# Two plain feed-forward pairs per layer, a state reload tied behind the last weight load, and one attention output product for both kv pairs, in a two-layer decoder step

## The chip, the cores and the metric

The kernel runs on one core of a Trainium2 chip. The metric is the device time of one execution in microseconds (us); three runs of the kernel before took 3076.03, 3079.45 and 3083.96 us, so its median is 3079.45 us. TensorE (PE) multiplies, VectorE (DVE), ScalarE (ACT) and GpSimd (POOL) work on the results, and SyncE (SP) issues the transfers; "PEld" is the loading of weights into TensorE, and "SPq" the queue of transfers that SyncE fills. Each engine works through its own instructions strictly in the order in which they stand, so an instruction that waits holds up all those behind it on the same engine.

## What is computed

One step of a two-layer decoder on 1024 prompt rows, 8 x 8 sample rows and 16 meta rows, 1104 columns in the kernel's transposed layout. Layer 0 is a state-space mixer with a feed-forward part, layer 1 is windowed attention with a feed-forward part, on 1088 columns (the meta rows have dropped out).

```python
def sq_relu_mlp(h, norm_w, w_up, w_down):
    return h + jnp.square(jax.nn.relu(rmsnorm(h, norm_w) @ w_up)) @ w_down

# layer 0
ym, conv_m, ssm_m = mamba_mixer(hm, zero_conv, zero_ssm, *prm)
...
# layer 1: keys and values shared, then queries, attention, output product
hp = hp + swa_prompt(q_p, k_p, v_p, k_meta, v_meta, attn_sinks[j]) @ w_o[j]
hs = hs + swa_sample(q_s, k_s, v_s, cache_k_win, cache_v_win, k_meta, v_meta, attn_sinks[j]) @ w_o[j]
...
hp = sq_relu_mlp(hp, mlp_norm_w[layer], w_up[layer], w_down[layer])
```

The model width is 1024, the hidden width of the feed-forward part 4096; there are 16 query heads and 4 key/value heads.

## The kernel before

**Three products for one.** Every float32 operand is split into a high part and a rest (`wh`, `wl` for weights, `xh`, `xl` for data), and `mm3` (L177 to L179) issues three matmuls for each 128-row slice. A weight comes in by a transfer into a `raw` buffer (two of them), ScalarE casts it to the high part (L162, or L853 for half-size pieces), GpSimd subtracts to get the rest (L163, L854); in layer 1 GpSimd first multiplies the queries' weights and the plain pairs' weights with a norm's weights (L160). There are six weight tiles `w` of 4 KB for each partition: a 128 x 1024 weight takes two of them, one for each part.

**Columns.** Work on the 1104 (1088) columns goes by three chunks of 384, 384 and 336 (320) columns. `S` holds the high parts and the rests of the stream, `g` names the single PSUM banks of the usual products, taken in a ring.

**Up projection.** The 4096 hidden columns are made in 16 pairs `f` of 2 x 128. A plain pair (`plain_up`) multiplies 8 slices x 3 matmuls for two halves and three chunks, 144 matmuls, and each result `g` is read out (ScalarE L833 in layer 0, VectorE L835 with the norm's factor in layer 1), squared (L836) and stored to DRAM (`r_d`, in layer 1 `r_e`). A block pair (`up_pair`) uses seven block products in place of eight, as Strassen's scheme does, on quarters of the columns (276 or 272 wide): 7 x 2 x 4 x 3 = 168 matmuls into four two-bank PSUM tiles `ma`, `mb`, `mc`, `md`, which VectorE (L882) and ScalarE combine. The weights of a block pair are sums that VectorE forms in `s` (L863, L869). The data of a block pair are sums too, which `sides` makes once a layer: differences of four slices over a quarter of the columns on VectorE (L795), the high part by ScalarE (L817) and the rest by VectorE (L818), six of them into tiles `T` and the others over the normed data in `S`. Those over `S` can be written only when no plain product reads that part of `S` any more. Before, pair 0 is plain and pairs 1 to 15 are block pairs.

**Between mixer and up projection in layer 0.** The last mixer products add into `hh` (L724), the squares of `hh` are summed in `acc`, a small product over all partitions (`ms`, L223 and L226) gives the norm's factor `rs` (two ScalarE functions, L234 and L235), then VectorE scales `hh` (L786), ScalarE writes the high part to `S` (L787) and VectorE the rest (L788), chunk by chunk. The plain pair starts on chunk 0 while chunk 2 is still being normed.

**Attention and its output product.** `attention` goes through chunks 0, 2, 1; for each, through two kv pairs `pr` and four query groups `r`; a step makes the next step's queries, then scores, softmax and weighted values for every 128 columns, with results in `ah` and `al` (eight buffers each). When four groups are done, four `out_unit` calls are noted down in `outs` and run at a later step; each loads one output weight, multiplies four slices (12 matmuls) into each of two `g` banks, and reads each bank out: two VectorE additions of the old `S` (L1319, L1320), a ScalarE cast (L1321) and a GpSimd or VectorE subtraction (L1322) back into `S`. For the second kv pair the sum goes on through `stream` (store to `h_e`, sum of squares in `acc`, L116). So each of the 24 column pieces (8 slices x 3 chunks) is read out twice, once for each kv pair. The last chunk's sum is kept in `X`; the other two chunks of `X` are loaded back from `h_e` (L126) and scaled with their norm factors (L136).

**Down projection.** Eight blocks of four 128-row slices; a block's data are read from `r_d`/`r_e` into `S` (L939), split on the chip (L944 cast, L945 rest), and its results are added to `hh` (L724). `hh` is reloaded from DRAM for this (L1487 in layer 0, L1555 in layer 1, eight transfers).

**Order.** The program is written in the order of the functions, and a scheduler at build time then fixes for each engine in which order its instructions stand, by dependences, priorities and free buffers. SyncE's transfers are fixed in the same way.

## Time and profile before

| what | value |
|---|---|
| median of three runs | 3079.45 us |
| the profiled execution | 3083.63 us, its span 3081.9 us |
| TensorE, mean granted clock | 0.979 |
| VectorE busy | 1751.6 us (57%) |
| ScalarE busy | 1377.2 us (45%) |
| GpSimd busy | 1253.1 us (41%) |
| moved by transfers | 305.87 MB, mean 99 GB/s |

The table is read from the top: the span is the profiled execution without what lies around its first and last instruction (1.7 us here). No engine but TensorE is busy for more than 57% of the span, but the shares differ from stage to stage: the up and down projections run from about 1090 to 1800 us (layer 0) and from about 2290 us to the end (layer 1), attention from about 1890 to 2276 us. Busy shares of TensorE are those of overlapping matmuls; how many matmuls stand in a stretch tells more.

### The profile page before, as it was taken

Reading aid. Unit: us, or ns where it says so; the run is one execution under the profiler, and the core shown is the slowest. Engines: PE = TensorE matmul, PEld = TensorE weight load, DVE = VectorE, ACT = ScalarE, POOL = GpSimd, SP = SyncE. Lnnn points to the kernel's source line nnn. Section 1 sums busy time; section 2 is a strip of 40 time slices with the busy share of each in tenths; the row PEclk is TensorE's granted clock in tenths of the full one; section 3 lists DMA queues with packets and bytes.
Section 4 is the critical chain, followed back from the end, with each engine's and each line's share of the span. In section 5 each row is a group of like instructions: output and inputs, shape, how many; then the busy total and the mean of one; then the engine's idle time right before and its main releaser. Section 6 shows DMA issues by size and latency. Waiting matters only on the chain.

```text
span 3081.9 us, 49051 instructions
## 1 busy us (share of the span) xinstructions
PE 2929.1 (95%) x19222; PEld 2796.9 (91%) x19222; DVE 1751.6 (57%) x3008; ACT 1377.2 (45%) x2606; POOL 1253.1 (41%) x1079
## 2 busy tenths in 40 slices
PE   6999999989999989999999999999987999999998
PEld 4988888879999979999999998887876999999998
DVE  5777877775555584332433356877886433423335
ACT  5455555555445554444221136656644544402113
POOL 4466666653333234443112145574532444312122
PEclk8999999999999999999999999999998999999999
DMA  3244444443222224234422212123232323512221
GB/s 128 68 118 119 119 115 117 128 134 130 73 67 75 78 76 132 89 112 154 149 100 78 71 42 63 64 90 99 80 108 85 107 96 114 194 55 99 107 71 66
DMA packets 189761, 305.87 MB, mean 99 GB/s; under 512 B 27528, under 2 KB 137480, under 8 KB 187464
## 3 DMA queue, kind: packets, MB, share of 16 engines
q1 hardware_dynamic: 189528, 302.72, 31.1%
q8 instruction: 151, 2.47, 0.3%
q14 instruction: 82, 0.67, 0.1%
HBM read 232.72 MB, written 70.92 MB: 99 GB/s over the span
## 4 chain that ended last, share of the span: by engine, by line
PE 49%; DVE 8%; ACT 3%; issue 3%; POOL 1%; DMA 1%; SPq 0%; DVEq 0%; ACTq 0%; POOLq 0%
PE g L178 9%; PE g L177 9%; PE g L179 9%; PE md L179 2%; PE md L178 2%; PE md L177 2%; PE mc L179 2%; PE mc L178 2%; PE mc L177 2%; PE ma L177 2%; PE ma L179 2%; PE ma L178 2%; PE mb L179 1%; PE mb L178 1%; PE mb L177 1%
## 5 line engine op out<-in xcount | busy, mean ns | idle before, releaser
L178 PE MATMUL g<-S,w 128*128 128x384 f32 (+2 forms) x2808 | 940.3, 335 | 9.5 <-DVE S L1322 4.7
L177 PE MATMUL g<-S,w 128*128 128x384 f32 (+2 forms) x2808 | 937.2, 334 | 11.4 <-DVE hh L724 3.8
L179 PE MATMUL g<-S,w 128*128 128x384 f32 (+2 forms) x2808 | 935.7, 333 | 0.0
L163 POOL TENSOR_TENSOR w<-raw,w 128x1024 fp32r<-128x1024 f32 x184 | 445.9, 2424 | 933.1 <-ACT w L162 866.3
L177 PEld LDWEIGHTS g<-S,w 128*128 128x128 f32 x2808 | 529.3, 188 | 19.6 <-DVE hh L724 4.0
L178 PEld LDWEIGHTS g<-S,w 128*128 128x128 f32 x2808 | 530.1, 189 | 17.3 <-DVE S L1322 5.3
L724 DVE TENSOR_TENSOR hh<-hh,g 128x384 f32<-128x384 f32 (+2 forms) x552 | 287.5, 532 | 445.0 <-PE g L179 444.3
L179 PEld LDWEIGHTS g<-S,w 128*128 128x128 f32 x2808 | 530.5, 189 | 6.2 <-issue 3.5
L162 ACT CAST w<-raw 128x1024 fp32r<-128x1024 f32 x184 | 192.5, 1046 | 603.6 <-PE g L178 575.1
L854 POOL TENSOR_TENSOR w<-s,w 128x512 fp32r<-128x512 f32 x120 | 166.3, 1390 | 332.3 <-ACT w L853 332.3
L532 DVE SCALAR_TENSOR_TENSOR fm<-xp,cv,fm 128x1024 f32<-128x1024 f32 x96 | 165.4, 1724 | 31.7 <-ACT fm L513 31.2
L854 POOL TENSOR_TENSOR w<-raw,w 128x512 fp32r<-128x512 f32 x90 | 123.1, 1369 | 95.1 <-ACT w L853 64.5
L177 PE MATMUL ma<-S,w 128*128 128x276 f32 (+1 forms) x480 | 139.7, 291 | 15.1 <-DVE n L835 13.8
L179 PE MATMUL ma<-S,w 128*128 128x276 f32 (+1 forms) x480 | 139.4, 290 | 0.0
L178 PE MATMUL ma<-S,w 128*128 128x276 f32 (+1 forms) x480 | 139.1, 290 | 0.0
L177 PE MATMUL g<-gh,w 128*128 128x384 f32 (+1 forms) x384 | 126.9, 332 | 2.4 <-DVE gt L696 1.1
L178 PE MATMUL g<-gl,w 128*128 128x384 f32 (+1 forms) x384 | 126.6, 330 | 0.0
L179 PE MATMUL g<-gh,w 128*128 128x384 f32 (+1 forms) x384 | 126.2, 330 | 0.0
L585 ACT ACTIVATE dec<-ab,acs 128x128 f32<-128x128 f32 (+1 forms) x288 | 90.8, 387 | 67.8 <-PE y L594 64.3
L863 DVE TENSOR_TENSOR s<-raw 128x512 f32<-128x512 f32 x60 | 50.1, 854 | 118.8 <-DMA raw<-in_w_up_dram 90.0
L177 PEld LDWEIGHTS ma<-S,w 128*128 128x128 f32 x480 | 91.1, 190 | 15.7 <-DVE n L835 14.1
L630 POOL TENSOR_TENSOR yt<-yt,yo 128x256 f32<-128x256 f32 (+1 forms) x72 | 68.2, 948 | 88.6 <-DVE yt L627 82.2
(390 smaller groups left out, 6891.8 us busy)
## 6 DMA issues: line engine op xcount, KB each, us to landing
raw<-in_w_up_dram SPq DMA_DIRECT2D x64, 512.0 KB
raw<-in_w_down_dram SPq DMA_DIRECT2D x64, 512.0 KB
raw<-in_w_in_dram SPq DMA_DIRECT2D x48, 512.0 KB
ab<-acs_d SPq DMA_DIRECT2D x64, 256.0 KB
S<-r_e SPq DMA_DIRECT2D x28, 544.0 KB
S<-r_d SPq DMA_DIRECT2D x24, 552.0 KB
raw<-in_w_q_dram SPq DMA_DIRECT2D x24, 512.0 KB
raw<-in_w_o_dram SPq DMA_DIRECT2D x24, 512.0 KB
```

The source lines that it names most:

```text
L162: nc.scalar.copy(out=wh, in_=raw)
L163: nc.gpsimd.tensor_tensor(out=wl, in0=raw, in1=wh.bitcast(F32), op=ALU.subtract)
L177: mm(out=out, lhsT=wh, rhs=xh, start=(first and k == 0), stop=False)
L178: mm(out=out, lhsT=wh, rhs=xl, start=False, stop=False)
L179: mm(out=out, lhsT=wl, rhs=xh, start=False, stop=(k == n - 1))
L532: nc.vector.scalar_tensor_tensor(out=acc[:, :SEQ], in0=xp[:, k:k + SEQ], scalar=cv[:, j, k:k + 1], in1=acc[:, :SEQ], op0=ALU.mult, op1=ALU ...
L585: nc.scalar.activation(out=dec[:n, h, :n], in_=ab[:n, h, :n], func=AF.Relu, scale=-1.0, bias=self.acs[:n, t, 4 * g + h:4 * g + h + 1])
L630: nc.gpsimd.tensor_tensor(out=yt[:, :, :no], in0=yt[:, :, :no], in1=yo[:, :, :no], op=ALU.add)
L724: nc.vector.tensor_tensor(out=hv, in0=hv, in1=pt[:, :n], op=ALU.add)
L854: nc.gpsimd.tensor_tensor(out=t[:, 1], in0=src, in1=t[:, 0].bitcast(F32), op=ALU.subtract)
L863: add = lambda a, b, op: (lambda t: (nc.vector.tensor_tensor(out=t, in0=a, in1=b, op=op), t)[1])(self.wsum([P] + sh))
```

## The change

1. In each layer pairs 0 and 1 are plain, and `up` starts at pair 2. A plain pair now yields once a chunk instead of once a result.
2. In layer 1 the tiles `T` come from one pool of six (before, two pools of three on the two sides of the memory), and the steps of `sides` stand elsewhere in the program: those of the first half of the blocks after the first chunk of pair 0, the others behind pair 0 and ahead of pair 1.
3. `hh` is reloaded by `load_stream`, with an ordering edge behind the last `raw` weight load of the up projection.
4. For chunks 0 and 2 the output product is made once for both kv pairs: an `out_unit` loads two weights (four of the six weight tiles) and multiplies eight slices (24 matmuls) into each bank, and the bank is read out once. Chunk 1 stays as it was. The noted units now also run one at a time at the steps of the first kv pair. `ah` and `al` have twelve buffers.

```diff
-                yield
+            yield
...
-        self.nc.sync.dma_start(out=t, in_=view)
+        self.last_raw = self.nc.sync.dma_start(out=t, in_=view).ins
...
-            for f in range(1, 16):
+            for f in range(2, 16):
...
+    def load_stream(self, big, h_d):
+
+        with self.tc.issue_after(self.last_raw):
+            for u in range(KT):
+                self.nc.sync.dma_start(out=big[:, u], in_=h_d[:, u])
...
-            if r == 3:
-                while outs:
+            if r == 3 or pr == 0 and outs:
+                for _ in range(len(outs) if r == 3 else 1):
                     self.out_unit(*outs.pop(0))
...
-                oc, opr = (c, pr) if sp is None else (2, sp)
-                outs += [(oc, chs[oc][1], opr, v, [a[oc, 4 * opr + q] for q in range(4)], xs, stream)
-                         for v in range(4)]
+                oc, prs = (c, (pr,)) if sp is None else (2, (sp,))
+                if oc != 1:
+                    prs = prs[0] * (0, 1)
+                if prs:
+                    outs += [(oc, chs[oc][1], prs, v, [a[oc, 4 * e + q] for e in prs for q in range(4)], xs, stream)
+                             for v in range(4)]
...
-        wh, wl = self.wunit(self.i["w_o"][pr, v], 4, 256)
+        ws = [self.wunit(self.i["w_o"][pr, v], 4, 256) for pr in prs]
+        last = prs[-1] == 1
...
-            self.mm3(pt, [(wh[:, k, ms], wl[:, k, ms]) for k in range(4)], [tuple(e[:, :n] for e in x) for x in a])
+            self.mm3(pt, [(wh[:, k, ms], wl[:, k, ms]) for wh, wl in ws for k in range(4)],
+                     [tuple(e[:, :n] for e in x) for x in a])
...
+                    for _ in self.plain_up(0, 1, dict(enumerate(CH)), rd):
+                        pass
...
-            for u in range(KT):
-                nc.sync.dma_start(out=big[:, u], in_=h_d[:, u])
+            self.load_stream(big, h_d)
...
-                for i in (1, 2, 3):
-                    step(i, 0)
...
                 next(plain)
+                for i in (1, 2, 3):
+                    step(i, 0)
                 stream.norm(1)
+                for _ in plain:
+                    pass
                 for i in (1, 2, 3):
                     step(i, 1)
-                for _ in plain:
+                for _ in self.plain_up(1, 1, {c: chs[c] for c in (0, 2, 1)}, rd, stream.rs, pre):
                     pass
```

Three places show what the scheduler made of it.

TensorE in layer 0, where the plain products end; before, `g_11404` and `g_11433` are the last results of pair 0, with weights `w_11244` and `w_11250`, and the first block product `ma` follows:

```order
L178 MATMUL g_11404<-S_90,w_11244 128x336
L179 MATMUL g_11404<-S_90,w_11245 128x336
L178 MATMUL g_11433<-S_90,w_11250 128x336
L179 MATMUL g_11433<-S_90,w_11251 128x336
L177 MATMUL ma_11512<-S_90,w_11509 128x276
L178 MATMUL ma_11512<-S_90,w_11509 128x276
```

Now pair 1 follows, whose results are `g_11503` and `g_11532` (chunks 0 and 1), with its own weights `w_11470` and `w_11464`:

```order
L178 MATMUL g_11404<-S_90,w_11244 128x336
L179 MATMUL g_11404<-S_90,w_11245 128x336
L178 MATMUL g_11433<-S_90,w_11250 128x336
L179 MATMUL g_11433<-S_90,w_11251 128x336
L177 MATMUL g_11503<-S_90,w_11470 128x384
L178 MATMUL g_11503<-S_90,w_11470 128x384
L177 MATMUL g_11532<-S_90,w_11464 128x384
```

So 120 of pair 1's 144 matmuls now stand between the end of pair 0 and the first block product (24 stand further up).

VectorE in layer 1, at the end of the plain pairs; `n3` are the read-out plain results, `S` and `T` the sums for the block pairs, `s` the first summed weight of the first block pair. Before:

```order
L818 TENSOR_TENSOR S_90<-X_22717,S_90 128x4x272 x2
L818 TENSOR_TENSOR T_23012<-t1_22935,T_23012 128x1088
L835 SCALAR_TENSOR_TENSOR n3_23135<-g_23110,acc_22760 128x384
L835 SCALAR_TENSOR_TENSOR n3_23164<-g_23139,acc_22760 128x384
L818 TENSOR_TENSOR T_23016<-X_22717,T_23016 128x1088
L795 TENSOR_TENSOR t1_22935<-X_22717,t1_22935 128x1088
L818 TENSOR_TENSOR T_23020<-t1_22935,T_23020 128x1088
L795 TENSOR_TENSOR t1_22935<-X_22717,t1_22935 128x1088
L818 TENSOR_TENSOR S_90<-t1_22935,S_90 128x4x272
L863 TENSOR_TENSOR s_23235<-raw_23203 128x512
```

Now:

```order
L818 TENSOR_TENSOR S_90<-X_22579,S_90 128x4x272
L818 TENSOR_TENSOR S_90<-t0_22796,S_90 128x4x272
L835 SCALAR_TENSOR_TENSOR n3_23156<-g_23131,acc_21338 128x320
L818 TENSOR_TENSOR S_90<-X_22579,S_90 128x4x272
L835 SCALAR_TENSOR_TENSOR n3_23185<-g_23160,acc_22622 128x384
L818 TENSOR_TENSOR S_90<-X_22579,S_90 128x4x272
L835 SCALAR_TENSOR_TENSOR n3_23214<-g_23189,acc_22622 128x384
L818 TENSOR_TENSOR S_90<-t1_22797,S_90 128x4x272
L818 TENSOR_TENSOR S_90<-X_22579,S_90 128x4x272 x2
L863 TENSOR_TENSOR s_23285<-raw_23253 128x512
```

The sums into `T` now stand further up, and behind pair 1's last result there are three sums into `S` ahead of `s`.

SyncE at the end of layer 1's up projection; `raw` from `in_w_down` are down-projection weights, `S` from `r_e2`, `r_e3`, ... the first blocks' data, `r_e15` from `rx` the last block pair's store, `hh` from `h_e` the reload. Before:

```order
L939 DMA S_90<-r_e4_18013 128x1088
L939 DMA S_90<-r_e2_18011 128x1088
L918 DMA r_e15_18024<-rx_26360 256x1x544
L939 DMA S_90<-r_e2_18011 128x1088
L939 DMA S_90<-r_e3_18012 128x1088 x2
L939 DMA S_90<-r_e4_18013 128x1088
L939 DMA S_90<-r_e5_18014 128x1088
L919 DMA r_e15_18024<-rx_26360 256x1x272
L920 DMA r_e15_18024<-rx_26360 256x1x272
L939 DMA S_90<-r_e5_18014 128x1088
L158 DMA raw_26992<-in_w_down_dram 128x1024
L1555 DMA hh_26602<-h_e_18025 128x1088 x8
```

Now:

```order
L158 DMA raw_26532<-in_w_down_dram 128x1024
L919 DMA r_e14_17984<-rx_25958 256x1x272
L920 DMA r_e14_17984<-rx_25958 256x1x272
L158 DMA raw_26624<-in_w_down_dram 128x1024
L940 DMA hh_26427<-h_e_17986 128x1088 x8
L158 DMA raw_26716<-in_w_down_dram 128x1024
L945 DMA S_90<-r_e4_17974 128x1088
L945 DMA S_90<-r_e2_17972 128x1088
L918 DMA r_e15_17985<-rx_26185 256x1x544
L945 DMA S_90<-r_e2_17972 128x1088
L945 DMA S_90<-r_e3_17973 128x1088 x2
```

The reload has moved from behind the first blocks' data to ahead of them. In layer 0 it stood there already before the change, and the order there is the same in this respect.

More of the change, by code (lines that the diff above doesn't have):

```diff
@@ L1321, in out_unit @@
             nc.scalar.copy(out=xh, in_=h)
-            (nc.vector if c == 1 and pr else nc.gpsimd).tensor_tensor(out=xl, in0=h, in1=xh.bitcast(F32),
-                                                                      op=ALU.subtract)
-            if pr:
+            (nc.vector if c == 1 and last else nc.gpsimd).tensor_tensor(out=xl, in0=h, in1=xh.bitcast(F32),
+                                                                        op=ALU.subtract)
+            if last:
                 stream.done(c, u, h)
@@ L1499, in second_layer @@
         qw = META // 4
-        sides = lambda pool: pool.tile([P, 2, 4, qw], F32R, tag="T", bufs=3, name="T")
-        with ExitStack() as cl:
+        with ExitStack() as cx:
             cr = ExitStack()
@@ L1524, in second_layer @@
             cr.close()
-            tr = self.pool("TR", ctx=cr, right=True)
+            tp = self.pool("T", ctx=cr, right=True)
             with ExitStack() as ce:
@@ L1553, in second_layer @@
             hts = [big[:, :, o:o + n] for o, n in chs]
-            for u in range(KT):
-                nc.sync.dma_start(out=big[:, u], in_=h_d[:, u])
+            self.load_stream(big, h_d)
             bufs = [R0] + self.halves(META) * 4
```

11 lines of the change are left out of this document (4 added, 7 removed).

## The prediction

> **What bounds the kernel now.** I read the page's engine table and its forty slices first, then windows by stage, then the waits of TensorE in the windows that lose most, then the timeline of the engine waited for.
>
> ```profile
> span 3081.9 us, 49051 instructions
> PE 2929.1 (95%) x19222; PEld 2796.9 (91%) x19222; DVE 1751.6 (57%) x3008; ACT 1377.2 (45%) x2606; POOL 1253.1 (41%) x1079
> PE   6999999989999989999999999999987999999998
> ```
>
> TensorE is busy for 95% of the span, so the kernel pays for matmuls, plus a few stretches in which TensorE waits. The slices below 9 that bear on the change are the seam between mixer and up projection in layer 0 (1088 to 1181 us), the seam between attention and up projection in layer 1 (2286 to 2375 us), and, too short for a slice, the start of layer 1's down projection. What one matmul costs where nothing waits comes from windows (us from the span's start, length, busy time and count of TensorE, its weight loads, VectorE, ScalarE, GpSimd, then the granted clock, the DMA share and GB/s):
>
> ```profile
> 1223.60:1436.60 213.00, 213.00 (x1682) 213.00 (x1681) 73.93 (x90) 104.75 (x173) 91.85 (x72) 1.00 0.32 104
> 2395.71:2607.24 211.53, 211.53 (x1682) 211.53 (x1681) 75.93 (x93) 104.05 (x175) 91.78 (x71) 1.00 0.32 103
> 2700.00:2730.00 30.00, 30.00 (x183) 30.00 (x182) 8.13 (x16) 3.14 (x3) 6.01 (x3) 1.00 0.11 37
> ```
>
> The first two windows are ten block pairs each (1682 matmuls at 168 a pair): 21.30 us a pair in layer 0 and 21.15 in layer 1. The third is plain work at full width: 30.00/183 = 0.164 us a matmul. A plain pair's 144 matmuls are then 144 x 0.164 = 23.6 us. So **each pair that turns from block to plain costs 2.3 us (layer 0) and 2.5 us (layer 1)** of TensorE, and the change can win only by the waits that it covers.
>
> **Part 1 and 2, layer 0: one more plain pair.** The windows are pair 0, then the first two block pairs; behind them TensorE's waits in these two (total, times, longest) and two stretches of VectorE.
>
> ```profile
> 1088.84:1125.89 37.05, 28.67 (x146) 27.57 (x147) 27.48 (x46) 22.45 (x39) 7.75 (x3) 0.91 0.13 47
> 1125.89:1180.72 54.83, 45.90 (x338) 44.38 (x336) 41.01 (x33) 28.04 (x44) 29.77 (x15) 0.97 0.33 107
> ```
>
> ```profile
> PE mc L178 <- DVE T L818: 4.8, 2, 2.8
> PE g L177 <- DVE hh L724: 3.8, 1, 3.8
> PE md L177 <- DVE rx L882: 2.6, 1, 2.6
> ```
>
> ```profile
> 1113.38 3.92 DVE L786 SCALAR_TENSOR_TENSOR hh<-hh,nv,rs 128x336 f32<-128x336 f32 x8 [6.13 <-ACT rs L235]
> 1120.91 2.18 DVE L788 TENSOR_TENSOR S<-hh,S 128x336 fp32r<-128x336 f32 x5
> ```
>
> The two windows take 91.88 us for work of 23.6 + 2 x 21.30 = 66.2, a loss of 25.7. Now the same stretch holds two plain pairs and one block pair, 2 x 23.6 + 21.3 = 68.5. The sums that the block pairs waited for (4.8 on `T`, and the rest of 54.83 - 42.6 = 12.2) are then made beside pair 1: VectorE's 41.01 us of the second window have 120 more matmuls, 19.7 us, of cover, and pair 1 asks of it nothing, since ScalarE reads its results. What stays is what stands ahead of pair 1: the 3.8 us for `hh`; about 1.8 of the 3.3 us (37.05 x 0.09) that the clock of 0.91 costs; about 3 us in which chunk 2 waits for its norm (VectorE scales it from 1113.38 to about 1123 us, and only 24 of pair 1's matmuls stand ahead of it). New are about 1.3 us for the weight tiles of pair 1, which come free only with pair 0's last product and need a cast first, and 1 us for the first block pair's own sums: estimates from the weight rows further down. So 68.5 + 10.9 = 79.4 in place of 91.9, **a gain of 12 us**. Bounds: if the block pairs still wait as they do now, 68.5 + 20 = 88.5, a gain of 3; if only the 3.8 and the clock stay, 16.
>
> **Part 1 and 2, layer 1.** The same for the last output products and pair 0, then the first block pair.
>
> ```profile
> 2285.59:2341.77 56.18, 31.44 (x159) 29.41 (x158) 50.13 (x70) 25.24 (x35) 6.78 (x3) 0.82 0.15 50
> 2341.77:2374.55 32.78, 25.40 (x168) 24.83 (x169) 19.73 (x19) 14.87 (x24) 14.15 (x11) 0.79 0.28 95
> ```
>
> ```profile
> PE ma L177 <- DVE n L835: 13.8, 1, 13.8
> PE md L177 <- ACT w L853: 6.8, 1, 6.8
> PE g L177 <- DVE X L1319: 4.5, 2, 4.3
> ```
>
> ```profile
> 2285.65 8.08 DVE L136 SCALAR_TENSOR_TENSOR X<-X,nv,acc 128x384 f32<-128x384 f32 x8
> 2293.65 0.55 DVE L1319 TENSOR_TENSOR X<-g,S 128x384 f32<-128x384 f32 x1
> 2312.88 1.21 DVE L116 TENSOR_TENSOR acc<-acc,sq 128x384 f32<-128x384 f32 x2
> 2337.10 2.48 DVE L818 TENSOR_TENSOR S<-X,S 128x1088 fp32r<-128x1088 f32 x2
> 2340.71 1.01 DVE L835 SCALAR_TENSOR_TENSOR n<-g,acc 128x384 f32<-128x384 f32 x2
> 2350.28 1.28 DVE L863 TENSOR_TENSOR s<-raw 128x512 f32<-128x512 f32 x2
> ```
>
> Here VectorE is the bound: 50.13 of 56.18 us busy, while TensorE makes 159 matmuls. The sums of `sides` stand ahead of the read-outs (L835), so the first block product waits 13.8 us for a bank of pair 0, and then 6.8 for its weight sums. With a further 21.15 for the second block pair, 110.1 us are used for 23.6 + 2.0 (12 output matmuls) + 42.3 = 67.9, a loss of 42.2. Now the work is 47.2 + 2.0 + 21.15 = 70.4, and VectorE's sums have pair 1's 23.6 us beside them; pair 1 adds six read-outs of 0.5 us to it. What stays: 8.6 us before the last output product (the scaling by L136, 8.08, and the read-out L1319, 0.55, stand ahead of it on VectorE; of this 4.3 shows as a wait now, because plain matmuls stood in the gap that now stand behind it); about 2 of the low clock; about 4.3 until the sum of squares is ready (it ends at 2314.1, and TensorE has run out of chunk 0 and 2 by about 2310); 1.3 for weight tiles as in layer 0; and the last read-out (0.5), three sums (3.7), the summed weight (1.28) and its rest on GpSimd (1.39), some 7, ahead of the first block product. That is 23.2, and 70.4 + 23.2 = 93.6 in place of 110.1: **a gain of 16 us**. Bounds: the 8.6 counted again behind the sums and the 13.8 back, a loss of 2; none of the waits behind the output product, a gain of 30. I take the middle because VectorE's work between 2286 and 2375 (69.9 us) fits into 93.6 but leaves little.
>
> ```profile
> L854 POOL TENSOR_TENSOR w<-s,w 128x512 fp32r<-128x512 f32 x120 | 166.3, 1390 | 332.3 <-ACT w L853 332.3
> ```
>
> (Of a group of instructions: count, total and mean in ns, idle time before them and what ended it; the 1390 is the rest on GpSimd used above.)
>
> **Part 3, the reload.** In layer 1 the eight loads of `hh` were issued behind the first blocks' data; in layer 0 they stood ahead already. The start of the down projection in each:
>
> ```profile
> 1440.00:1470.00 30.00, 29.08 (x208) 28.89 (x207) 7.54 (x12) 12.07 (x16) 8.48 (x4) 1.00 0.76 287
> 2670.00:2700.00 30.00, 23.24 (x128) 22.92 (x127) 16.66 (x18) 11.22 (x12) 4.91 (x2) 0.89 0.98 372
> ```
>
> ```profile
> PE g L177 <- DVE hh L724: 6.8, 1, 6.8
> 2681.32 8.52 SPq L1555 DMA_DIRECT2D hh<-h_e  x8
> 1448.92 4.01 SPq L1487 DMA_DIRECT2D hh<-h_d  x8
> 2687.09 3.90 DVE L945 TENSOR_TENSOR S<-S 128x1088 fp32r<-128x1088 f32 x2 [0.65 <-ACT S L944]
> 2690.99 3.24 DVE L724 TENSOR_TENSOR hh<-hh,g 128x384 f32<-128x384 f32 x7
> ```
>
> In layer 1 30 us hold 128 matmuls where 183 would fit: 55 x 0.164 = 9.0 us lost, 6.8 of it in a wait for the banks that L724 reads once `hh` is there. In layer 0 the same stretch is idle for 0.9. With layer 0's order the gain is 9.0 - 0.9, less some tenths for first blocks' data that come later: **7.7 us**. Bounds: 8.5 above; below, the reload's 4.46 MB (8 x 128 x 1088 x 4 bytes) at the 372 GB/s of this stretch hold the queue for 12 us, and if all of that reached the blocks the gain would be -3. I take the value near layer 0, the nearest row: the edge fixes the same place.
>
> The Trainium skill, "DMA: Bandwidth & Descriptors", section "Queues, rings and completion order", speaks against this part: on each SDMA engine descriptors are consumed in ring order, so what is queued first is served first and the blocks' data stand behind the reload. By that rule alone the 12 us fall on the blocks and the 7.7 is lost; layer 0's 0.92 idle us (30.00 - 29.08) behind the same order speak for enough lead.
>
> **Part 4, the output product.** Of 48 read-outs (24 pieces, two kv pairs) the 16 first ones of chunks 0 and 2 go.
>
> ```profile
> 1890.00:2276.00 386.00, 357.83 (x2523) 317.57 (x2522) 308.98 (x784) 237.55 (x630) 211.65 (x175) 0.97 0.26 84
> PE yb L1183 <- DVE mb L1178: 11.3, 10, 2.0
> PE g L177 <- DVE hs L1319: 3.2, 4, 1.8
> L1319 DVE TENSOR_TENSOR hs<-g,S 128x384 f32<-128x384 f32 x24 | 13.0, 546 | 0.2
> L1320 DVE TENSOR_TENSOR hs<-hs,S 128x384 f32<-128x384 f32 x24 | 19.7, 826 | 0.4
> ```
>
> No matmul goes. VectorE loses 16 x (0.55 + 0.83) = 22 us of its 309. TensorE idles 386 - 357.8 = 28.2 us there, of which the two waits on VectorE in the rows, 14.5 us, can shrink; VectorE's work is spread over the stretch and 22 of 309 is 7%, so I take a bit under half of these waits, **6 us**. Bounds: 15 (all of them); -10, if the units, which take four weight tiles at once, hold up TensorE for two of their preparations (rows below).
>
> **Sum.** 12 + 16 + 7.7 + 6 = 41.7. The profiled execution took 3083.63, so the change makes 3041.9 of it; the median of the runs shown, 3079.45, lies 4.2 lower, and 3079.45 - 41.7 = **3038 us**.
>
> **Rivals.** *VectorE stays the bound in layer 1's seam*: the first block product's wait for the banks (L835) comes back behind pair 1, as 50.13 of 56.18 speaks for it, and the sums ordered ahead of the read-outs against it; gain of that seam nil, 3038 + 16 = 3054. *The reload holds up the first blocks' data*, or stands where it did: the reload gains nothing or loses a little, 3038 + 12 = 3050 at worst. *Attention loses 12 in place of gaining 6*: the noted units run at fewer steps, and blocks without a unit beside them wait for the softmax on VectorE (the 11.3 us row); 3038 + 18 = 3056. *Slower, by the six weight tiles*: a unit now holds four of them, so the next weight of the queries has none free until the unit's last product, and its preparation shows:
>
> ```profile
> L160 POOL TENSOR_TENSOR raw<-raw,nv 128x1024 f32<-128x1024 f32 x16 | 31.5, 1970 | 10.5 <-DMA raw<-in_w_q_dram 7.4 <-DVE es L1141 3.1
> L162 ACT CAST w<-raw 128x1024 fp32r<-128x1024 f32 x37 | 38.6, 1044 | 8.1 <-PE g L178 4.6 <-DMA raw<-in_w_o_dram 3.3
> L163 POOL TENSOR_TENSOR w<-raw,w 128x1024 fp32r<-128x1024 f32 x37 | 89.9, 2433 | 40.6 <-ACT w L162 21.1 <-DVE es L1141 12.2 <-DVE vt L1074 2.9
> ```
>
> One preparation is 1.97 + 1.04 + 2.43 = 5.45 us. There are 16 such weights; all of them exposed are 87 us, so 3038 + 87 = 3125, and slower than before it is from the eighth on (41.7/5.45 = 7.7). Against it: the transfer and the norm's product need no `w`, and attention's own matmuls stand between.
>
> **Chances and range.** Forecast, 3026 to 3050: 0.58. VectorE in layer 1: 0.12. Reload: 0.10. Attention loses: 0.11. Slower by weight tiles: 0.04. Better than the forecast, all parts near their upper bounds: 0.05. The likeliest gives the number, 3038. The upper end takes in the rivals at 3050, 3054 and 3056 with 4 us for their own spread, 3060; the lower takes half of the upper bounds' excess (4 + 14 + 0.8 + 9 = 28, half 14, and 6 for spread), 3018. A measurement of this kernel tells about 0.3%, 9.2 us, from no change: of the 0.33 of the three middle rivals I put 0.06 on two of them coming together (3038 + 16 + 18 = 3072), which is within 0.3%; so faster, below 3070.2, has 0.58 + 0.05 + 0.27 = 0.90, within it 0.06, slower 0.04.
>
> **What would show it.** Right: in layer 0 no wait of `mc` for `T` and no more than 1 us before the first block pair's `md`; in layer 1 no wait of `ma` for `n` above 2 us, and pair 1 without gaps; 30 us at the start of layer 1's down projection with 170 matmuls or more, and `hh` issued ahead of the first blocks' data; attention with VectorE about 22 us lighter and TensorE's idle time nearer 22 than 28. Wrong: the 13.8 us wait behind pair 1, gaps of 5 us ahead of queries' products, or the first blocks' cast (L944) late.

## The result and the profile after

| | before | after |
|---|---|---|
| median (four runs each) | 3081.60 us | 3060.11 us |
| lowest to highest | 3076.03 to 3083.96 | 3052.12 to 3061.72 |
| profiled execution, span | 3081.9 us | 3059.9 us |

The ratio is 0.9928, with a 95% interval of 0.9904 to 0.9951: the change is faster by 0.7%, 21.5 us by the medians. A gain of 41.7 us was forecast, so the sign was right and the gain half of it. On the prediction's base of 3079.45 us the ratio gives 3057 us: outside the forecast of 3026 to 3050, and at the end of the range that was kept for the rivals, none of which came as described.

The span and the engine table of the page after (busy us, share of the span, instructions):

```profile
span 3059.9 us, 48866 instructions
PE 2935.1 (96%) x19174; PEld 2804.4 (92%) x19174; DVE 1723.2 (56%) x2964; ACT 1368.0 (45%) x2578; POOL 1234.6 (40%) x1055
```

TensorE is busy for 6.0 us more than before in a span that is 22.0 shorter. It makes 48 matmuls fewer, but a plain pair takes some 3 us longer than a block pair (24.3 and 21.3 us in layer 0), and the waits have gone down by more than that. The windows of the stretches that the prediction speaks of (us from the span's start, length, busy time and count of TensorE, weight loads, VectorE, ScalarE, GpSimd, then granted clock, DMA share and GB/s). Before, layer 0's seam, attention, layer 1's seam:

```profile
1088.66:1180.72 92.06, 74.74 (x484) 71.96 (x482) 68.67 (x78) 50.67 (x82) 37.70 (x18) 0.94 0.25 83
1891.09:2275.00 383.91, 356.11 (x2513) 315.86 (x2512) 307.82 (x781) 237.29 (x629) 211.18 (x174) 0.97 0.26 84
2275.00:2395.71 120.71, 88.22 (x552) 85.35 (x552) 88.15 (x108) 54.74 (x81) 35.92 (x22) 0.86 0.28 96
```

Now, with layer 0's seam cut at the first block product, and with 30 us from 1 us ahead of the end of layer 1's pair 15 as the last row:

```profile
1091.40:1155.25 63.85, 53.95 (x293) 52.90 (x291) 42.52 (x56) 36.36 (x62) 16.68 (x7) 0.92 0.19 64
1155.25:1176.73 21.48, 21.48 (x170) 21.44 (x169) 15.67 (x13) 12.20 (x19) 13.01 (x8) 1.00 0.46 169
1886.84:2269.83 382.99, 357.65 (x2513) 317.43 (x2512) 287.62 (x749) 231.44 (x613) 193.16 (x159) 0.97 0.25 80
2269.83:2381.56 111.73, 91.49 (x528) 89.04 (x528) 95.64 (x107) 50.79 (x75) 43.28 (x19) 0.89 0.35 118
2655.96:2685.96 30.00, 29.18 (x178) 28.96 (x178) 17.64 (x22) 12.57 (x13) 7.70 (x3) 1.00 0.80 317
```

Each stretch is bounded by the same TensorE work in both traces, and pairs are named by their number `f`:

| stretch | before | after | difference | forecast |
|---|---|---|---|---|
| layer 0, end of the mixer's products to the start of pair 3 | 92.06 | 85.33 | -6.7 | -12 |
| attention, first score to last weighted value | 383.91 | 382.99 | -0.9 | -6 |
| layer 1, last weighted value to the start of pair 3 | 120.71 | 111.73 | -9.0 | -16 |
| layer 1, end of pair 15 to the last matmul | 403.32 | 395.34 | -8.0 | -7.7 |

Up to the end of the mixer's products, where TensorE has the same order in both, the trace after runs 2.7 us late (over all fourteen traces of this document that point lies between 1086.99 and 1091.40 us); with that the four differences make the 22.0.

The first block pair of layer 0 now waits for nothing: 21.48 us, the second row. What is left stands ahead of it. TensorE's waits after in layer 0's seam, and then in layer 1's (total, times, longest):

```profile
PE g L177 <- DVE hh L724: 4.8, 1, 4.8
PE g L177 <- ACT S L787: 2.6, 1, 2.6
PE g L179 <- POOL w L163: 1.8, 1, 1.8
PE g L177 <- ACT w L162: 0.7, 1, 0.7
```

```profile
PE g L177 <- DVE X L1331: 7.6, 2, 4.7
PE g L223 <- ACT msh L221: 6.7, 1, 6.7
PE md L177 <- ACT w L853: 2.7, 1, 2.7
PE mc L177 <- DVE rx L882: 2.5, 1, 2.5
```

The 13.8 us for `ma` of before are gone. In its place the wait ahead of the norm's small product (L223) has grown to 6.7 us; before, it was this:

```profile
PE g L223 <- ACT msh L221: 1.7, 1, 1.7
```

How the granted clock answers to such waits is in windows of 4 us around pair 0's start in layer 0 (same columns):

```profile
1092.00:1096.00 4.00, 0.00 (x0) 0.00 (x0) 3.96 (x3) 2.20 (x3) 3.59 (x2) 0.90 0.53 174
1096.00:1100.00 4.00, 3.58 (x11) 3.58 (x12) 1.78 (x4) 2.83 (x4) 0.00 (x0) 0.50 0.54 172
1100.00:1104.00 4.00, 4.00 (x19) 4.00 (x19) 4.00 (x9) 2.84 (x7) 0.00 (x0) 0.74 0.03 8
1104.00:1108.00 4.00, 4.00 (x25) 4.00 (x23) 4.00 (x9) 2.30 (x6) 0.00 (x0) 1.00 0.14 49
```

TensorE waits 4.85 us, and then works at a clock of 0.50, half speed, for 5.6 us: 11 matmuls start in the second window, which holds 24 to 25 at full clock. Such matmuls count as busy, so this loss shows in no wait and in no busy share; it shows in the granted clock and in the count.

### The profile page after: what moved, and what is told of

Read it like the earlier page. It is cut to its first block, busy times and chain, and to the rows that moved or that the text cites. A ratio compares the mean times of both kernels' runs of the same rounds, so it can differ in the third digit from the quotient of the medians.

```text
span 3059.9 us, 48866 instructions
## 1 busy us (share of the span) xinstructions
PE 2935.1 (96%) x19174; PEld 2804.4 (92%) x19174; DVE 1723.2 (56%) x2964; ACT 1368.0 (45%) x2578; POOL 1234.6 (40%) x1055
## 4 chain that ended last, share of the span: by engine, by line
PE 52%; DVE 7%; ACT 3%; issue 2%; POOL 1%; DMA 0%; DVEq 0%; POOLq 0%; ACTq 0%
PE g L177 10%; PE g L178 10%; PE g L179 10%; PE md L179 2%; PE mc L179 2%; PE md L178 2%; PE mc L177 2%; PE mc L178 2%; PE md L177 2%; PE ma L179 2%; PE ma L177 2%; PE ma L178 2%; PE mb L179 1%; POOL w L163 1%; PE mb L178 1%
## 5 line engine op out<-in xcount | busy, mean ns | idle before, releaser
L177 PE MATMUL g<-S,w 128*128 128x384 f32 (+2 forms) x2904 | 971.9, 335 | 17.5 <-DVE hh L724 4.8
L178 PE MATMUL g<-S,w 128*128 128x384 f32 (+2 forms) x2904 | 974.4, 336 | 2.8 <-DVE S L317 2.2
L179 PE MATMUL g<-S,w 128*128 128x384 f32 (+2 forms) x2904 | 968.2, 334 | 1.8 <-POOL w L163 1.8
L163 POOL TENSOR_TENSOR w<-raw,w 128x1024 fp32r<-128x1024 f32 x188 | 463.6, 2468 | 983.2 <-ACT w L162 924.1
L177 PEld LDWEIGHTS g<-S,w 128*128 128x128 f32 x2904 | 549.7, 189 | 26.3 <-issue 5.8
L178 PEld LDWEIGHTS g<-S,w 128*128 128x128 f32 x2904 | 550.2, 189 | 10.0 <-DVE S L317 3.2
L179 PEld LDWEIGHTS g<-S,w 128*128 128x128 f32 x2904 | 550.7, 190 | 8.2 <-issue 3.6
L724 DVE TENSOR_TENSOR hh<-hh,g 128x384 f32<-128x384 f32 (+2 forms) x552 | 288.3, 533 | 440.7 <-PE g L179 439.9
L854 POOL TENSOR_TENSOR w<-s,w 128x512 fp32r<-128x512 f32 x112 | 150.4, 1346 | 252.3 <-ACT w L853 251.4
L854 POOL TENSOR_TENSOR w<-raw,w 128x512 fp32r<-128x512 f32 x84 | 113.4, 1351 | 90.6 <-ACT w L853 56.6
L179 PE MATMUL ma<-S,w 128*128 128x276 f32 (+1 forms) x448 | 129.5, 289 | 0.0
L177 PE MATMUL ma<-S,w 128*128 128x276 f32 (+1 forms) x448 | 129.5, 289 | 0.0
L177 PE MATMUL g<-gh,w 128*128 128x384 f32 (+1 forms) x384 | 126.9, 332 | 2.5 <-DVE hh L724 1.2
L178 PE MATMUL ma<-S,w 128*128 128x276 f32 (+1 forms) x448 | 129.1, 288 | 0.0
L1143 ACT ACTIVATE es<-es,few 128x273 f32<-128x273 f32 (+2 forms) x136 | 70.9, 526 | 55.3 <-DVE few L1141 41.4
```

Of the source, the lines that this page charges most:

```text
L163: nc.gpsimd.tensor_tensor(out=wl, in0=raw, in1=wh.bitcast(F32), op=ALU.subtract)
L177: mm(out=out, lhsT=wh, rhs=xh, start=(first and k == 0), stop=False)
L178: mm(out=out, lhsT=wh, rhs=xl, start=False, stop=False)
L179: mm(out=out, lhsT=wl, rhs=xh, start=False, stop=(k == n - 1))
L724: nc.vector.tensor_tensor(out=hv, in0=hv, in1=pt[:, :n], op=ALU.add)
L854: nc.gpsimd.tensor_tensor(out=t[:, 1], in0=src, in1=t[:, 0].bitcast(F32), op=ALU.subtract)
```

## The experiments

Each is a kernel of its own, timed beside before. "Stretch" below means a row of the table above, read in the same way from that kernel's trace.

| kernel | median, us | ratio to before, 95% interval |
|---|---|---|
| before + second plain pair | 3057.79 | 0.9922 (0.9908 to 0.9937) |
| before + the reload's edge | 3082.63 | 0.9998 (0.9989 to 1.0008) |
| before + merged output product (T in one pool) | 3071.33 | 0.9971 (0.9958 to 0.9984) |
| after without the merged output product | 3059.12 | 0.9927 (0.9910 to 0.9943) |
| before + T in one pool | 3073.03 | 0.9969 (0.9956 to 0.9981) |
| after, half of pair 1 ahead of chunk 2 | 3055.17 | 0.9910 (0.9896 to 0.9925) |
| after, sums behind the norm in layer 1 | 3049.54 | 0.9893 (0.9878 to 0.9908) |
| after, 24 matmuls in the wait | 3055.62 | 0.9916 (0.9901 to 0.9931) |
| after, 60 free matmuls in the wait | 3051.36 | 0.9899 (0.9884 to 0.9914) |
| half of pair 1 ahead, rests on VectorE | 3045.42 | 0.9882 (0.9866 to 0.9899) |
| sums and scaling behind the norm | 3048.21 | 0.9886 (0.9872 to 0.9901) |
| the last two together | 3033.20 | 0.9848 (0.9832 to 0.9864) |

Medians alone don't separate the kernels with small edits to the changed kernel: the one with 24 matmuls in the wait has a longer stretch (below) and still a median 4.5 us under the changed kernel's, whose four runs spread over 9.6 us. What an edit did is therefore read from its stretch.

### The parts, one at a time

The second plain pair alone (with the pool for `T` and the place of the sums that come with it in the diff):

> The second plain pair alone (both layers, with T in one pool and the sums where the change has them), without the reload's edge and with an output product for each kv pair. Theory A, the parts are additive and each is worth what its stretch of the changed kernel's trace shows: layer 0 from the end of the mixer's products to the third block pair's start 7 us shorter, layer 1 from attention's last product to the same place 9 us shorter, together 16 us, ratio 0.995. Rival B, the merged output product made room for the pairs in layer 1 (VectorE has 22 us less to do): without it layer 1's gain falls under 4 us and the kernel gains less than 11.

It gives the whole gain, 24 us by the medians, more than either theory. In its trace layer 0's stretch is 85.70 us, layer 1's 109.91, and the stretch behind pair 15, which it was not to touch, 395.86 in place of 403.32. So about 7.5 us of it were what the prediction had booked on the reload's edge.

The reload's edge alone (`load_stream` and `last_raw` in before):

> The edge of the reload alone, one plain pair a layer. Theory A: 8 us less, all of it in layer 1 between the last block pair's end and the end of the kernel, ratio 0.9974. Rival B, the reload's 4.46 MB delay the first blocks' data here as these are no longer covered: under 3 us.

Nothing: 0.9998. SyncE's queue at the end of layer 1's up projection in this kernel (start, us, transfers):

```profile
2673.17 3.60 SPq L945 DMA_DIRECT2D S<-r_e  x5
...
2680.42 0.33 SPq L945 DMA_DIRECT2D S<-r_e  x1
2681.66 0.34 SPq L158 DMA_DIRECT2D raw<-in_w_down_dram  x1
2682.97 8.53 SPq L940 DMA_DIRECT2D hh<-h_e  x8
```

The reload stands behind the first blocks' data as in before. The edge says "not ahead of the last `raw` load", and that was already so; it does not pull anything forward. The order of instructions is the same as before's on all five engines.

The merged output product alone. It needs the room that `T` in one pool leaves, so the pool came with it:

> The output product for both kv pairs alone (with T in one pool, for which the twelve buffers of ah and al make the room necessary). Theory A, its 22 us of VectorE lie off the path: within 2 us of before. Rival B: it gains 4 to 6 us inside attention, which the changed kernel loses again elsewhere.

It came out 9 us faster (0.9971), more than either theory, and its trace, which is that of the fastest of its eight runs (3066.01 to 3080.80 us), shows 6.9 of it behind pair 15 again, 396.43 us. Attention is 379.08 us there, 4.8 less than before's, which lies within what traces of the same attention differ by (last section). That left `T`'s pool as what this kernel and the one with the pairs have in common. The same seen from the other side, the changed kernel without the merged product:

> The changed kernel without the merged output product (two read-outs a piece as before). Theory A: as the changed kernel within 2 us, 3058 to 3062 by its profiled execution. Rival B: 4 us or more slower, in layer 1's seam.

As theory A had it: 0.9927 against 0.9928, with intervals that would hide some 5 us. This kernel and the one with the second pair alone differ by the edge only, and have the same order on every engine too.

### What moved the reload

```diff
-            tl = self.pool("TL", ctx=cl)
...
-            tr = self.pool("TR", ctx=cr, right=True)
+            tp = self.pool("T", ctx=cr, right=True)
```

> Before with one change: the six tiles T come from one pool on the right side. Theory A, this and not the edge moved the reload: from the last block pair's end of layer 1 to the last matmul 6.5 to 8 us less than before (403.3 us there), hh issued ahead of the first blocks' data, and nothing else, so about 7 us in all, ratio 0.9977. Rival B, it needs the merged output product or the second plain pair too: under 2 us there.

Theory A held, with somewhat more than its 6.5 to 8 us. The end of its up projection on SyncE:

```profile
2659.50 3.96 SPq L1551 DMA_DIRECT2D hh<-h_e  x8
2665.17 0.33 SPq L158 DMA_DIRECT2D raw<-in_w_down_dram  x1
2667.30 0.80 SPq L939 DMA_DIRECT2D S<-r_e  x2
```

Pair 15 ends at 2668.5, so the reload now starts 9 us ahead of that end; in before it started 10 us behind it. The stretch behind pair 15 is 393.99 us, 9.3 less than before's, and the median falls by 9.1. The changed kernel has the early reload too (`2647.93` there, 9.0 us ahead of pair 15's end at 2656.96). VectorE's order in layer 1's seam also changes a little with the pool, but that stretch is as long as before's (120.72 and 120.71 us). Which tile of the old layout shared its memory with `hh`, so that the reload was put late, was not tried apart from this.

### The wait in the middle of layer 0's plain pairs

TensorE's order in the changed kernel has one matmul for each of pair 0's two banks of chunk 2, then 24 of pair 1 that could run, then the rest of chunk 2. The first of them waits for the high part of chunk 2 (2.6 us), and the 24 stand behind it.

```diff
...
+                    self.plain_one(0, w0, 1, chd, rd)
+                    w1 = self.plain_ws(0, 1, (0,))
+                    for c in (0, 1):
+                        self.plain_one(1, w1, c, chd, rd)
+                    self.plain_one(0, w0, 2, chd, rd)
+                    self.plain_one(1, w1, 2, chd, rd)
+                    w1 = self.plain_ws(0, 1, (1,))
...
```

> The changed kernel with, in layer 0, the first half of pair 1 on chunks 0 and 1 written ahead of pair 0's chunk 2: 48 of pair 1's matmuls ahead of chunk 2, and no matmul of chunk 2 ahead of them. Theory A, the wait of 2.6 us for chunk 2's high part holds ready work behind it on TensorE's queue, and costs about as much again by the lower granted clock after it: 4 to 5 us less from the end of the mixer's products to the second block pair's start (85.3 us in the changed kernel). Rival B, chunk 2's norm waits for something that comes later in the same measure, so it saves under 1.5 us.

A miss. The 2.6 us are gone, but layer 0's stretch is 85.18 us, as long as before the edit (85.33): another wait has taken its place. TensorE's waits in it, and GpSimd's row at that time:

```profile
PE g L177 <- DVE hh L724: 4.8, 1, 4.8
PE g L179 <- POOL w L163: 4.5, 1, 4.5
```

```profile
1130.93 8.50 POOL L163 TENSOR_TENSOR w<-raw,w 128x1024 fp32r<-128x1024 f32 x1 [36.69 <-PE g L179]
```

The six weight tiles hold three halves of pairs, so pair 1's second half can be prepared only when pair 0 is done. Its rest takes GpSimd 8.50 us, where L163 has a mean of 2.43 in the prediction's rows. At that time VectorE makes the sums of `sides`, one right behind the other until 1137.2:

```profile
1134.71 2.52 DVE L818 TENSOR_TENSOR T<-hh,T 128x1104 fp32r<-128x1104 f32 x2
```

The rest ends at 1139.4, 2.2 us after the last of these sums. That is about the time that a rest takes by itself, which speaks for its getting its turn only when VectorE paused.

### VectorE and GpSimd hold each other up

The same meeting stands ahead of pair 0 in the changed kernel. VectorE and GpSimd there, timeline:

```profile
1090.30 0.50 DVE L778 TENSOR_TENSOR acc<-acc,n 128x336 f32<-128x336 f32 x1
1090.71 0.50 DVE L724 TENSOR_TENSOR hh<-hh,g 128x336 f32<-128x336 f32 x1
1091.13 4.83 DVE L778 TENSOR_TENSOR acc<-acc,n 128x336 f32<-128x336 f32 x2
1095.88 0.49 DVE L724 TENSOR_TENSOR hh<-hh,g 128x336 f32<-128x336 f32 x1
```

```profile
1090.39 5.20 POOL L163 TENSOR_TENSOR w<-raw,w 128x1024 fp32r<-128x1024 f32 x2 [31.42 <-ACT w L162]
```

Two additions that take 0.5 us each elsewhere take 4.83 together (2.26 and 2.53) while GpSimd works on its two rests, and the second ends at 1095.96, just behind GpSimd's end at 1095.59; both read two operands on the chip's SBUF, whereas L724 beside them, with one operand in PSUM, keeps its 0.5. The last L724 is late by that, and TensorE's bank with it: these are the 4.85 us. If the two engines hold each other up, taking GpSimd's part away helps; if they only meet by chance, VectorE has 4.8 us more to do (the expectation below has 4.4 us for L778; it is the 2.26 and 2.53 above). The edit lets VectorE make the four rests, on top of the one above:

```diff
-        nc.gpsimd.tensor_tensor(out=wl, in0=raw, in1=wh.bitcast(F32), op=ALU.subtract)
+        (by or nc.gpsimd).tensor_tensor(out=wl, in0=raw, in1=wh.bitcast(F32), op=ALU.subtract)
...
+        by = None if layer else self.nc.vector
```

> e_half with the rests of the four plain weights of layer 0 made by VectorE instead of GpSimd. Theory A, VectorE's and GpSimd's operations from SBUF hold each other up (L778 takes 4.4 us beside GpSimd's L163, L163 7.6 to 8.5 us beside VectorE's sums): without them the wait ahead of pair 0 falls from 4.85 to under 3 us, the one of 4.5 us inside pair 1 under 2 us, and from the mixer's end to the second block pair's start it is 4 us or more shorter than e_half's 85.2 us. Rival B, the two engines only meet by chance: VectorE has 4.8 us more to do, the sums come late and nothing is gained.

Theory A, and by more than it asked: layer 0's stretch is 74.74 us, 10.4 less. Its waits from the mixer's last products to pair 3 (L892 is L882 of before), VectorE's row of one rest, and the window up to the first block product:

```profile
PE g L177 <- DVE hh L724: 1.7, 1, 1.7
PE mc L177 <- DVE rx L892: 1.5, 1, 1.5
PE g L223 <- ACT msh L221: 0.6, 1, 0.6
```

```profile
1090.40 1.23 DVE L163 TENSOR_TENSOR w<-raw,w 128x1024 fp32r<-128x1024 f32 x1
```

```profile
1088.30:1139.89 51.59, 49.38 (x291) 48.88 (x291) 40.34 (x59) 33.51 (x57) 13.45 (x3) 1.00 0.23 77
```

A rest costs VectorE 1.23 us, the additions of L778 are back at 0.51 us each, no wait is longer than 1.7, and the clock is 1.00 throughout: 51.59 us for 291 matmuls, where the changed kernel took 63.85 for 293.

### The half clock after a wait

Two kernels put matmuls that nobody reads into the wait ahead of pair 0. The first took a bank from the new ring:

```diff
...
+                    for _ in range(24):
+                        self.tc.keep_in_program_order(nc.tensor.matmul(out=g[:, :384], lhsT=w0[0][:, 0], rhs=w0[0][:, :3], start=True, stop=True))
```

> The changed kernel with 24 matmuls more, which nobody reads (a weight by itself into a bank of its own), in TensorE's wait of 4.85 us ahead of pair 0 in layer 0. Theory A, a wait of some us is followed by some 5 us at half the granted clock (matmuls 320 ns apart and not 176): with the wait filled the first matmuls of pair 0 are 176 ns apart, and the stretch from the mixer's end to pair 0's 40th matmul is 2 to 2.5 us shorter in spite of the additional matmuls. Rival B, the clock falls with something else (the load on the transfers or VectorE), and the stretch is as long as before or longer.

It says nothing on the question: the bank was one that waited for the same read-outs, so the additional matmuls themselves waited 4.84 us and came behind the wait instead of in it; layer 0's stretch grew to 87.26 us. The second takes a bank of the mixer's ring that is free, and operands that are always there:

```diff
+                g = self.gps()
+                for _ in range(60):
+                    self.tc.keep_in_program_order(nc.tensor.matmul(out=g[:, :P], lhsT=self.ones_r, rhs=self.ones_r, start=True, stop=True))
```

> The changed kernel with 60 short matmuls (128 columns, read by nobody) that wait for nothing, in TensorE's wait ahead of pair 0 in layer 0 (4.85 us). Theory A, the half clock follows the wait: filled up, pair 0's first matmuls come 176 ns apart and not 320, and the stretch from the mixer's last product to pair 0's 40th matmul is 2 us or more shorter. Rival B, the clock falls for another reason: the first twenty matmuls stay 320 ns apart.

Its windows of 4 us (same columns):

```profile
1088.00:1092.00 4.00, 4.00 (x38) 4.00 (x37) 3.96 (x2) 0.78 (x1) 4.00 (x2) 1.00 0.51 176
1092.00:1096.00 4.00, 4.00 (x33) 4.00 (x33) 1.87 (x4) 3.01 (x4) 0.07 (x1) 1.00 0.54 172
1096.00:1100.00 4.00, 4.00 (x25) 4.00 (x24) 2.53 (x5) 3.62 (x7) 0.00 (x0) 1.00 0.07 29
```

The clock stays at 1.00, and pair 0's matmuls are 176 ns apart from the first on, against 320 for 16 of them in the changed kernel. So the half clock follows the wait: theory A held in this. The stretch to pair 0's 40th matmul fell by 0.9 us only (14.49 to 13.54), not by the 2 expected: the 60 took 6.66 us and themselves put pair 0 off by 1.7; layer 0's stretch is 84.31. The Trainium skill, "TensorE: Matmul & The Clock Gate", Part 1, has a clock gate that opens and closes with TensorE's activity in a window of some 3.4 us that runs freely. The trace agrees that it is activity, and that it is not always the same: the wait of 2.6 us for chunk 2 was followed by 11 slow matmuls in the changed kernel, by 2 in the kernel with sums and scaling behind the norm.

The fourteen traces together show how far this can be relied on. From 60 us on they hold 93 waits of TensorE of 2.7 us or more, and each had the half clock within 4 us of its end. Of the shorter waits that stand alone, a stretch of half clock began close to 9 of 17 of 2.4 to 2.7 us, 9 of 27 of 1.8 to 2.4 us, 21 of 115 of 1.0 to 1.8 us and 1 of 240 below that (alone: no other wait of 0.3 us within 7 us; close: from 3.5 us ahead of the wait to 4 us behind it). Apart from the start and the end of the program, the half clock lasted 3.4, 6.8, 10.2 or 13.7 us; in the changed kernel it was 6.8 from 1095.2 us and 3.4 from 1119.1.

### VectorE's order in layer 1's seam

In the changed kernel six sums of the first half of the blocks (L795, L818, 1.28 us each, 7.7 together) stand on VectorE ahead of L222, which prepares the last chunk's norm, and five of them ahead of the end of that chunk's sum of squares (L116), for which TensorE waits 6.7 us. The last of them:

```profile
2311.86 1.21 DVE L116 TENSOR_TENSOR acc<-acc,sq 128x384 f32<-128x384 f32 x2
2313.11 1.29 DVE L818 TENSOR_TENSOR T<-t,T 128x1088 fp32r<-128x1088 f32 x1
2314.31 0.55 DVE L222 TENSOR_TENSOR msl<-acc,msh 128x384 fp32r<-128x384 f32 x1
```

```diff
-                for i in (1, 2, 3):
-                    step(i, 0)
                 stream.norm(1)
+                with self.tc.issue_after(self.stat_lo):
+                    for i in (1, 2, 3):
+                        step(i, 0)
```

(`stat_lo` is the instruction of L222.)

> The changed kernel with, in layer 1, VectorE's sums of the first half of the blocks queued behind the last chunk's sum of squares (L222 on VectorE). Theory A, these 9 us of sums stand ahead of the norm's chain and make the wait of 6.7 us before the small product and the half clock after it: the wait falls under 1 us, and from attention's end to the second block pair's start it is 6 to 8 us shorter (111.7 us in the changed kernel). Rival B, VectorE is the bound of the whole seam, so the sums then come late for the first block pair, whose waits grow by as much: under 2 us gained.

Theory A: the wait of 6.7 us ahead of L223 is gone, and the longest waits of TensorE in the seam are now

```profile
PE g L177 <- DVE X L1331: 7.5, 2, 4.6
PE md L177 <- ACT w L853: 3.7, 1, 3.7
```

and the stretch is 101.64 us, 10.1 less than in the changed kernel's trace and 7.5 less than the mean of 109 of the five traces with the changed kernel's layer 1 (106.0 to 111.7). The first block pair waits for 3.7 us in place of 2.7 and 2.5, so little of rival B shows. The next edit moves the scaling of chunks 0 and 2 (L136) behind L222 as well:

> e_sums_late with the scaling of chunks 0 and 2 (L136, 11 us of VectorE) queued behind the last chunk's sum of squares as well. Theory A, the scaling stands ahead of the last output products' read-outs, so their wait of 4.6 us and the one of 2.9 us behind it go, and layer 1's seam (101.6 us in e_sums_late from attention's end to the second block pair's start) is 5 us shorter or more. Rival B, VectorE now makes 20 us of scaling and sums behind the norm, more than it has free beside the plain pairs: the first block pair waits for its sums and the seam is as long or longer.

Between the two: the waits of 7.5 us for L1331 fall to 1.0, but the stretch to 99.55, 2.1 and not 5 shorter. TensorE now reaches pair 0 before its weights are made (in this kernel the lines stand two lower, so L175 is `mm3`'s L177, L160 the cast, L161 its rest and L1329 the read-out L1331):

```profile
PE g L175 <- ACT w L160: 4.0, 2, 2.3
PE md L175 <- ACT w L851: 2.5, 1, 2.5
PE g L177 <- POOL w L161: 2.2, 1, 2.2
PE g L175 <- DVE X L1329: 1.0, 2, 0.5
```

By the medians the two kernels cannot be told apart.

### Both seams together

> e_rest's layer 0 and e_scale_late's layer 1 together. Theory A, the two are in different stretches and add up: from the mixer's last product to the third last block pair 287.7 us as in e_rest (298.3 in the changed kernel), from attention's end to the third last block pair of layer 1 about 311 (323.5), together some 22 us less than the changed kernel, ratio to before about 0.985, 3036 us. Rival B, one of the two was helped by where its run happened to lie (attention alone varies by 8 us between runs of one order): under 15 us less than the changed kernel.

It beats both kernels: 3033.20 us, 26.9 less than the changed kernel. Layer 0's stretch is 74.55, layer 1's 100.13, each as in the kernel that it comes from. Against the changed kernel's trace these are 10.8 and 11.6 us less, the 22 that theory A named; what is more lies mostly where TensorE has the same order in both (attention is 3.9 us shorter, the mixer ends 3.6 us earlier); the edits don't explain that part, and it is counted as luck of these runs.

## Why the prediction was right in sign and half in size

**Plain pair, layer 0: forecast -12, measured -6.7.** The mechanism was right: the waits of the first block pairs for `T` went, and pair 0's and pair 1's lengths are on the path. The step that was mis-sized is the sum of what stays, 10.9 us. It measured 85.33 - 68.5 = 16.8. Of this the first wait is 4.85 for the 3.8 taken; the weights 2.5 (0.7 and 1.8) for 1.3; the plain matmuls 1.4 (at full clock 176 ns for 384 columns and 154 for 336, so a pair of layer 0 is 96 x 0.176 + 48 x 0.154 = 24.3 us, not 23.6, which came from layer 1's widths); and the largest error was the clock. "About 1.8 of the 3.3 us" was taken to stay, without a reason for the 1.8, and the 0.97 of the second window, another 1.6 us, was left out. In the trace after, TensorE works at half clock for 9.0 us of this stretch, which loses 4.5; before, it was 10.1 and 5.0. So the clock's part stayed almost whole: the half clock behind the wait for `T` went, but the longer first wait and the one for chunk 2 bring as much. Over more traces the gain is smaller still: the other three with before's order here have 88.75 to 89.61, the five with the changed order 85.33 to 85.71.

**Plain pair, layer 1: forecast -16, measured -9.0.** The waits named as removed were removed, and the rival with `ma` waiting for `n` behind pair 1 did not come. Predicted was a rest of 23.2. By the same count from 2285.59 us, which is 10.6 behind attention's last value, the stretch was to be 104.2, and is 111.7. The waits that stay were nearly right one by one (7.6 for 8.6 at the last output product, 5.2 for 7 at the first block pair, 6.7 for 4.3 at the norm). The term that failed is again "about 2 of the low clock": the 528 matmuls take 91.49 us, some 81 at full clock (288 plain at 0.166, 168 block in 21.15, 72 others at 0.174), so the clock costs 9 to 10 (18.0 us of work at half clock, 9.0 lost, where before lost 8.2). The prediction gives no working for its 2, beside rows with clocks of 0.82 and 0.79. The kernel with the sums moved shows that the 6.7 was a matter of VectorE's order and not of its load. The changed kernel's trace is the longest of its kind here: the other four with its layer 1 have 105.98 to 109.90 us and the other three with one plain pair there 118.96 to 121.56, so the gain is nearer 11 than 9.

**Reload: forecast -7.7, measured -8.0, for a wrong reason.** The size came from comparing with layer 0, and holds; that the change had this gain at all is luck as far as its working goes. The step that failed is "the edge fixes the same place": the edge moved nothing, and the pool of `T`, which the prediction took for a detail of the plain pairs, moved the reload. The order of a kernel with all parts shows what stands where; it does not show which part put it there. The rival from ring order did not come: no wait for the first blocks' data shows in the 36 us behind pair 15's end, and the 30 us window above holds 178 matmuls of 183.

**Output product: forecast -6, measured -0.9.** VectorE is 20 us lighter there, about as counted (307.8 to 287.6 us between the same two places), but TensorE idles 25.3 us in place of 27.8, and not nearer 22 as the prediction's sign had it. The step "a bit under half of these waits" failed: TensorE's waits for VectorE in the row `mb` fell from 11.3 to 3.2 us, and waits for other steps of the softmax took their place:

```profile
PE yb L1176 <- DVE es L1147: 3.5, 2, 3.1
PE yb L1189 <- DVE mb L1184: 3.2, 5, 1.2
```

The timed pair without and with it gives 0.9927 and 0.9928; one more, `T`'s pool without and with it, 0.9969 and 0.9971. Nine traces with the merged product have 381.5 us on average, five without 383.5, in a spread of 8 us. So a gain of 2 us is possible and one of 6 is not borne out. The rival of weight tiles did not come either: no wait for `w` stands among TensorE's waits there.

**The sum.** The four were added as if each were certain at its middle; the two seams came out at a little over half and attention at a sixth, and the two seams shared one cause, the half clock behind the waits that stay.

## What to carry to other kernels

In these traces a wait of TensorE of 2.7 us or more always had matmuls at half clock behind it, mostly for 3 to 6 us in the two seams, so it costs there some 1.5 to 3 us more than its length; price it so, and count matmuls in a window rather than its busy share. Before an ordered engine's work is called too much, look at what stands ahead of the one instruction that others wait for: 8 us of sums moved behind L222 gained more than a 20 us lighter VectorE did. And where several edits change one order, take each alone: an edge that only forbids moves nothing forward, and the layout of the memory may be what does.

## What the hardware showed beside this

VectorE and GpSimd hold each other up when both read two operands in SBUF: L778 2.26 and 2.53 us in place of 0.5, L163 7.58 us in the changed kernel and 8.50 in an experiment in place of 2.43. The additions of L778 ended right behind GpSimd's rests, and L163 2.2 us behind the last of VectorE's sums in both kernels, which speaks for taking turns and not for a shared rate. With the rests on VectorE the waits behind them were gone. The Trainium skill, "GPSIMD Engine Reference", section "Key points", states that the two share their SBUF interfaces; these rows agree.

Attention took between 377.9 and 385.9 us in the eight traces of the changed kernel and of those that keep its attention and change other places only, although TensorE has the same order there in all eight. The granted clock goes with it: it was 0.98 in the shortest and 0.95 in the longest, where TensorE worked at half clock for 17.1 and 36.5 us, while its idle time differs by 1.3 us. So the same program meets the half clock more often in one run than in the next; what decides that was not tried.
